# A hybrid S5 and gated-delta block on one Trainium2 core: S5 factors kept on chip, half of a copy on GpSimd, gate tiles queued behind read-outs

## The chip, the cores and the metric

The kernel runs on one core of one Trainium2 chip, in fp32 with fp32r and fp16 matmuls where the kernel splits values. The metric is device time in microseconds of one launch. Three runs of the kernel before gave 928.39, 932.23 and 933.82 us; their median is 932.23 us.

## The reference, cut to what matters

One layer: adaLN modulation, one input projection, two groups of heads, one output projection, LayerNorm. The change lies in the S5 group, which handles 512 of the 1024 mixed columns as 32 groups of 16 channels with 64 complex states, in two directions.

```
abar = exp(lam * dt);  bbar = ((abar - 1) / lam) * B          # per direction
h[t] = abar * h[t-1] + bbar @ u[t]                            # scan, started from the context's state
y    = d_skip * u + sum over both directions of Re(C @ h)
out  = glu(gelu(y)) * silu(z)                                 # z: the gate columns of the projection
```

The other group is a gated delta rule with a 3x3 convolution ahead of it and its own silu gate. The sequence has 1024 latent tokens after 256 context tokens.

## The kernel before, in words

The scan is cut into chunks of 8 tokens. Within a chunk the output is a Toeplitz product of the inputs (tile `m8`, built from kernels in DRAM `d_k`), and what comes from earlier chunks is the state at the chunk's edge (`ebuf`, copied to `hq`) times factors C·abar^t (tile `f`). Four S5 stages matter here:

- The **unfold** (lines 701 to 706, VectorE) completes the states in `ebuf`.
- The **Toeplitz stage** `s5_toeplitz` (lines 415 to 452), `t0` to `t3`, each for two quads of four groups. It loads packed coefficients `spq` from `d_sp`, makes `f` in six VectorE products a quad (`cplx_chunk`, lines 406 to 411), stores `f` to DRAM `d_f` (line 429), multiplies it with C on TensorE (line 442) into `ka` and `kb`, copies these to `ktt` and stores `ktt` to `d_k` (line 450).
- The **read-out** `y_stage` (lines 831 to 874), `y0` to `y3`, each for eight groups. It loads `m8` in eight pieces from `d_k` (line 837), `u8` (line 841) and two `fq` from `d_f` (line 845), copies the states to `hq` (line 848: the lower 64 partitions forwards, the upper 64 backwards in time), runs 24 fp32 matmuls into `py` (lines 854 to 856), the GELU on ScalarE (line 857), eight transposes `pg` and the copies to `gT`, stored to `d_g` (line 871).
- The **gate tiles** `z_tile` (lines 818 to 824), `z0` to `z7`. Each loads 128 columns of the input projection (`wrz`), splits them in high and low parts (`wtz`, lines 724 and 725), runs 48 matmuls of 128x512 (`pjz`, lines 142 to 144), and stores the silu (`csz`) to `d_z`.

After them come the GLU (`w`: its weights `wgr` split into `wgt`; `g`: matmuls `pgl`) and, in memory that the projection's operands leave, the delta-rule part, whose first instructions are `mg` on GpSimd (line 1188).

Order. The program is traced in an order written by hand, `ORD` (line 1103), and a planner then places each engine's instructions by priority in that order and by its own costs. `issue_after` puts the block's instructions behind a given one on that one's engine only. DMA issues stand in the queues of the engine that issues them (Q is SP, S is ScalarE), each in order. SBUF tiles share slots by tag: `kk`, `ra` and `ac` have two, `u4` four, `wr4` two, `w8` two (split projection weights), `y4` four. In the trace, slots of a tag are handed out in the order of the program. `ktt` and `csz` are in `kk`, `f` and `hq` in `ra`, the product's scratch, `ysb` and `gT` in `ac`, `spq` and the GLU's split weights in `u4`; `m8`, `u8` and `fq` are in `u4` for even and in `y4` for odd read-outs. `wrz`, `wgr` and the `zts` of the GLU use `wr4`.

Of the kernel before, what the change touches and what calls it, by code (L numbers as in the profile page):

```python
# [9 lines left out]
F32 = mybir.dt.float32  # L10
# [4 lines left out]
AF = mybir.ActivationFunctionType  # L15
# [4 lines left out]
P = 128  # L20
# [5 lines left out]
NG = 32  # L26
# [15 lines left out]
def tile_hybrid_block(  # L42
# [30 lines left out]
    V, S, G, T, Q = nc.vector, nc.scalar, nc.gpsimd, nc.tensor, nc.sync  # L73
# [12 lines left out]
    def bankE(nm):  # L86
        return psW.tile([P, 512], F32, tag="e", name=nm)
# [40 lines left out]
    d_uc = tc.dram_tile([CTX, 512], F32, name="d_uc")  # L128
    d_e = tc.dram_tile([P, NG, 2, P], F32, name="d_e")
    d_sp = tc.dram_tile([P, 8, 336], F32, name="d_sp")  # L130
    d_f = tc.dram_tile([P, NG, 2, P], F32, name="d_f")
    d_k = tc.dram_tile([NG, GC, 240], F32, name="d_k")
    d_kt = tc.dram_tile([HEADS, P, TOK], F32, name="d_kt")
    d_qkv = tc.dram_tile([3, HEADS, P, TOK], F32, name="d_qkv")
# [42 lines left out]
    def c5(shape, nm, tag):  # L177
        return cvp.tile(shape, F32, tag=tag, name=nm)
# [4 lines left out]
    def u4(nm, dt=F32, n=1024):  # L183
        return ld.tile([P, n], dt, tag="u4", name=nm, bufs=4)
# [214 lines left out]
    def cplx_chunk(cr, ci, pr, pi, conj, ch, tv, tg, E2):  # L399
        shp = [P, 4, 8, GC]  # L400
        cr, ci = bc(cr[:, :, None, :], shp), bc(ci[:, :, None, :], shp)
        pr = bc(pr.rearrange("p t g -> p g t")[:, :, :, None], shp)
        pi = bc(pi.rearrange("p t g -> p g t")[:, :, :, None], shp)
        vr = ch[:, :, 0, :].rearrange("p g (t c) -> p g t c", t=8)
        vi = ch[:, :, 1, :].rearrange("p g (t c) -> p g t c", t=8)
        V.tensor_tensor(vr, cr, pr, op=ALU.mult)
        V.tensor_tensor(tv, ci, pi, op=ALU.mult)
        V.tensor_tensor(vr, vr, tv, op=ALU.add if conj else ALU.subtract)
        E2.tensor_tensor(vi, ci, pr, op=ALU.mult)
        E2.tensor_tensor(tg, cr, pi, op=ALU.mult)  # L410
        E2.tensor_tensor(vi, vi, tg, op=ALU.subtract if conj else ALU.add)

    tz = {}

    def s5_toeplitz(q0, q1):
        for q in range(q0, q1):
            if q % 2 == 0:
                tz["k"] = c5([P, 2, 240], f"ktt{q}", "kk")
                tz["s"] = sq2 = u4(f"spq{q}", n=672)
                Q.dma_start(sq2, d_sp[:, q:q + 2].rearrange("p q f -> p (q f)"))  # L420
            kt = tz["k"]
            sq = tz["s"][:, (q % 2) * 336:(q % 2) * 336 + 336]
            ctt = [sq[:, 128 + 64 * i:192 + 64 * i].rearrange("p (j c) -> p j c", c=GC) for i in range(2)]
            fpp = [sq[:, 256 + 32 * i:288 + 32 * i].rearrange("p (t j) -> p t j", j=4) for i in range(2)]
            dd = sq[:, 320:336]
            f = c5([P, 4, 2, P], f"f{q}", "ra")
            ftmp = c5([P, 4, 8, GC], f"ft{q}", "ac")
            cplx_chunk(ctt[0], ctt[1], fpp[0], fpp[1], True, f, ftmp, ftmp, V)
            S.dma_start(d_f[:, q * 4:(q + 1) * 4], f)
            bank_ = bankW if q % 2 else bankE  # L430
            pa, pb = bank_(f"ka{q}"), bank_(f"kb{q}")
            for part in range(2):
                for lo, ps, cc0, f0, ft in ((0, pa, 0, 16, 0), (64, pb, 112, 0, 1)):
                    for ri in range(2):
                        for j in range(4):
                            w = sq[lo:lo + 64, 64 * ri + j * GC:64 * ri + j * GC + 32]
                            if part == 0:
                                o, m = ps[32 * j:32 * j + 32, cc0:cc0 + GC], ctt[ri][lo:lo + 64, j, :]
                            else:
                                o = ps[32 * j:32 * j + 32, f0:f0 + 112]  # L440
                                m = f[lo:lo + 64, j, ri, ft * GC:ft * GC + 112]
                            T.matmul(o, w, m, start=(ri == 0), stop=(ri == 1), tile_position=(lo, 32 * j))
            k2 = kt[:, q % 2, :]
            V.tensor_copy(k2[:, 128:240], pa[:, 16:128])
            V.tensor_tensor(k2[:, 112:128], pa[:, 0:16], dd, op=ALU.add)
            V.tensor_copy(k2[:, 0:112], pb[:, 0:112])
            V.tensor_tensor(k2[:, 112:128], pb[:, 112:128], k2[:, 112:128], op=ALU.add)
            if q % 2:
                for j in range(4):
                    S.dma_start(  # L450
                        d_k.rearrange("(q j) c f -> j c q f", j=4)[j][:, q - 1:q + 1], kt[32 * j:32 * j + GC],
                    )

# [254 lines left out]
    def chain(n0, n1):  # L708
        ar, ai = apw[2]
        for m in range(n0, n1, 4):  # L710
            prev, cur = ebuf[:, m - 4], ebuf[:, m]
            ta = rtp.tile([P, NG, 2], F32, tag="rta", name=f"rta{m}")
            tb = rtp.tile([P, NG, 2], F32, tag="rtb", name=f"rtb{m}")
            G.tensor_tensor(ta, prev, ar, op=ALU.mult)  # L714
            G.tensor_tensor(tb, prev[:, :, ::-1], ai, op=ALU.mult)
            G.tensor_tensor(ta, ta, cur, op=ALU.add)
            G.tensor_tensor(cur, ta, tb, op=ALU.add)
# [108 lines left out]
    d_g = tc.dram_tile([4, P, LAT], F32, name="d_g")  # L826
# [3 lines left out]

    def y_stage(ct):
        ysb = c5([P, 8, P], f"ysb{ct}", "ac")
        yt_ = u4 if ct % 2 == 0 else y4
        m8 = yt_(f"m8_{ct}").rearrange("p (g f) -> p g f", g=8)
        u8 = yt_(f"u8_{ct}").rearrange("p (g f) -> p g f", g=8)
        for s in range(8):
            Q.dma_start(
                m8[16 * s:16 * s + 16],
                d_k[ct * 8:ct * 8 + 8, :, (7 - s) * 16:(7 - s) * 16 + P].rearrange("g c f -> c g f"),
            )  # L840
        Q.dma_start(u8, d_ug[:, ct * 8:ct * 8 + 8])
        for q in range(2):
            g0 = ct * 8 + q * 4
            fq = yt_(f"fq{g0}").rearrange("p (g r f) -> p g r f", g=4, r=2)
            Q.dma_start(fq, d_f[:, g0:g0 + 4])
            hq = c5([P, 4, 2, P], f"hq{g0}", "ra")
            for lo, sl in ((0, slice(NCX - 1, NST - 1)), (64, slice(NST - 2, NCX - 2, -1))):
                S.activation(  # L848
                    hq[lo:lo + 64].rearrange("p g r n -> p n g r"), ebuf[lo:lo + 64, sl, g0:g0 + 4, :], AF.Copy,
                )  # L850
            py = bankE(f"py{g0}")
            for j in range(4):
                o = py[:, j * P:(j + 1) * P]
                T.matmul(o, u8[:, q * 4 + j], m8[:, q * 4 + j], start=True, stop=False)
                T.matmul(o, hq[:, j, 0, :], fq[:, j, 0, :], start=False, stop=False)
                ins = T.matmul(o, hq[:, j, 1, :], fq[:, j, 1, :], start=False, stop=True)
            S.activation(
                ysb[:, :, q * 64:(q + 1) * 64].rearrange("p t (g c) -> p g t c", c=GC),
                py.rearrange("p (g t c) -> p g t c", g=4, t=8), AF.Gelu,
            )  # L860
        gT = c5([P, LAT], f"gT{ct}", "ac")
        for h2 in range(2):
            pg = bankE(f"pg{ct}_{h2}")
            for j in range(4):
                T.transpose(pg[:, j * P:(j + 1) * P], ysb[:, h2 * 4 + j, :], ident)
            V.tensor_copy(
                gT.rearrange("p (n t) -> p t n", t=8)[:, h2 * 4:h2 * 4 + 4, :],
                pg.rearrange("p (t n) -> p t n", t=4),
            )
        if ct < 3:  # L870
            S.dma_start(d_g[ct], gT)
        else:
            marks["gT"] = gT
        return ins
# [221 lines left out]
    ebuf = epool.tile([P, NSL, NG, 2], F32, name="ebuf")  # L1096
# [3 lines left out]
        e_stage(hf)  # L1100
        fold(hf)
    chain(7, 35)
    ORD = "z0 t0 z1 z2 t1 y0 z3 t2 y1 z4 t3 y2 z5 y3 z6 w z7 g"
    for hd in range(HEADS):
        head(hd)
        if hd < 2:
# [8 lines left out]
    def y4(nm):  # L1115
        return yp.tile([P, 1024], F32, tag="y4", name=nm)
# [14 lines left out]
    marks = {}  # L1131
    for st in ORD.split():
        name, _, hold = st.partition(">")
# [308 lines left out]
    def gate_z(hd):  # L1442
        zt = gs.tile([P, LAT], F32, tag="zt", name=f"zt{hd}", bufs=1)
        Q.dma_start(zt, d_z[1, hd])
        return zt
# [195 lines left out]
    z3 = gate_z(HEADS - 1)  # L1641
# [37 lines left out]
```

## Time and profile before

| | |
|---|---|
| median of three runs | 932.23 us |
| the profiled execution | 937.24 us, its span 934.9 us |
| TensorE busy | 817.6 us (87%), mean clock 0.949 |
| VectorE, ScalarE, GpSimd busy | 668.6, 431.0, 372.5 us |
| HBM read, written | 85.53 MB, 41.23 MB |

Times on a timeline are microseconds from the span's start. The heads' convolutions end near 400; t0 to t3, y0 to y3 and the gate tiles lie between 379 and 539; the delta-rule part fills the rest. A matmul in fp32 over 128 columns appears as two instructions. The clock is the share of TensorE's full speed that was granted; a TensorE row's busy time overlaps the next one's start, so the distance of starts is the better price.

### The profile page before, as it was taken

The numbers are of one execution on the slowest core, as the hardware profiler recorded it, in microseconds if no ns is written. First come the engines' busy times: TensorE is split into PE (matmuls) and PEld (weight loads), VectorE is DVE, ScalarE is ACT, GpSimd is POOL, SyncE is SP. The second block draws the span as 40 slices with busy tenths as digits, with TensorE's granted clock in tenths as the row PEclk, the third lists the DMA queues.
The fourth block names the chain that finished last, engine by engine and source line by source line (L and its number), as shares of the span: only waits on it lengthen the run. The fifth ranks groups of instructions, "written<-read, shape, count | busy, mean of one in ns | idle before, by whom it ended". The sixth has DMA issues, their size and how long they took to land.

```text
span 934.9 us, 17192 instructions
## 1 busy us (share of the span) xinstructions
PE 817.6 (87%) x6553; PEld 675.7 (72%) x6553; DVE 668.6 (72%) x1318; ACT 431.0 (46%) x950; POOL 372.5 (40%) x455
## 2 busy tenths in 40 slices
PE   5987999997889999999894995799899989779994
PEld 2655897785776788877673884688777977677883
DVE  7977986996766778998432489677574765676576
ACT  1321435324434454421458475565743753456363
POOL 3224240007897930100000078875752773351063
PEclk9998999999898999999997897799999999899997
DMA  9980447412304323347546576421314224314423
GB/s 248 295 178 12 178 165 228 145 39 75 130 23 163 112 100 96 123 151 216 164 137 224 181 265 196 148 92 46 125 59 143 72 104 150 123 44 144 161 98 117
DMA packets 122427, 127.87 MB, mean 137 GB/s; under 512 B 21662, under 2 KB 95958, under 8 KB 122218
## 3 DMA queue, kind: packets, MB, share of 16 engines
q1 hardware_dynamic: 101898, 87.55, 32.5%
q10 hardware_dynamic: 20448, 39.23, 11.1%
q8 instruction: 52, 0.85, 0.4%
q14 instruction: 29, 0.24, 0.1%
HBM read 85.53 MB, written 41.23 MB: 136 GB/s over the span
## 4 chain that ended last, share of the span: by engine, by line
PE 53%; DVE 15%; DMA 13%; POOL 7%; ACT 5%; issue 5%; SPq 1%; ACTq 0%; POOLq 0%; DVEq 0%
PE pjz L142 3%; PE pjz L143 2%; PE pjz L144 2%; DMA xr<-in_x_dram 2%; PE pjk L142 2%; PE pjk L143 2%; PE pjk L144 2%; PE u L142 2%; DMA ml<-d_mix 2%; DMA kT<-d_qkv 2%; DMA wad<-in_w_ada_dram 2%; ACT hq L848 2%; PE pjv L143 2%; PE u L143 2%; PE pjv L144 2%
## 5 line engine op out<-in xcount | busy, mean ns | idle before, releaser
L1188 POOL TENSOR_TENSOR mg<-tri,ghi 128x512 fp32r<-128x512 f32 x20 | 23.1, 1157 | 196.9 <-PE pjz L144 153.9
L714 POOL TENSOR_TENSOR rta<-ebuf,ar 128x64 f32<-128x64 f32 x38 | 24.8, 653 | 85.4 <-DVE ebuf L689 82.6
L142 PE MATMUL pjz<-h_hi,wtz 128*128 128x512 f32 x128 | 52.1, 407 | 0.5 <-ACT csz L823 0.5
L143 PE MATMUL pjz<-h_lo,wtz 128*128 128x512 f32 x128 | 51.4, 402 | 0.0
L144 PE MATMUL pjz<-h_hi,wtz 128*128 128x512 f32 x128 | 51.1, 399 | 0.0
L1299 PEld LDWEIGHTS <-xz 128*128 128x128 f16 x480 | 37.2, 101 | 18.5 <-issue 12.4
L1283 DVE TENSOR_TENSOR pad<-pp,lvm 128x256 f16<-128x256 f32 x100 | 40.4, 416 | 13.1 <-PE pp L1275 12.5
L1299 PE MATMUL px<-pad,xz 128*128 128x64 f16 x480 | 42.0, 197 | 6.9 <-DVE pad L1283 5.3
L1312 DVE TENSOR_TENSOR xz<-px,xz 128x512 f16<-128x512 f32 x60 | 40.6, 684 | 9.7 <-PE px L1299 7.7
L760 DVE SCALAR_TENSOR_TENSOR cak<-crk,cwt,cak 128x945 f32<-128x945 f32 (+2 forms) x32 | 39.5, 1234 | 7.6 <-ACT cak L750 7.1
L1299 PE MATMUL px<-xz,pad 128*128 128x64 f16 x480 | 43.2, 197 | 0.0
L760 DVE SCALAR_TENSOR_TENSOR caq<-crq,cwt,caq 128x945 f32<-128x945 f32 (+2 forms) x32 | 39.2, 1224 | 5.0 <-ACT caq L750 3.1
L760 DVE SCALAR_TENSOR_TENSOR cav<-crv,cwt,cav 128x945 f32<-128x945 f32 (+2 forms) x32 | 39.8, 1243 | 3.7 <-ACT cav L750 3.4
L1275 PE MATMUL pp<-xz,t 128*128 128x64 f16 x480 | 33.7, 197 | 8.0 <-DVE xz L1312 3.5
L848 ACT ACTIVATE hq<-ebuf 64x1024 f32<-64x1024 f32 x16 | 31.9, 1991 | 13.0 <-DMA d_k<-ktt 8.4
L804 POOL TENSOR_TENSOR kss<-kss,mhalf 128x4 f32<-128x4 f32 (+1 forms) x12 | 15.6, 1307 | 55.1 <-DVE kss L803 55.1
L1275 PEld LDWEIGHTS <-t 128*128 128x128 f16 x480 | 27.9, 101 | 13.1 <-issue 11.5
L142 PE MATMUL u<-wu,h_lo 128*128 128x512 f32 x64 | 29.9, 468 | 8.3 <-DVE h_lo L563 8.3
L1400 ACT ACTIVATE uu<-s 128x128 f32<-128x128 f32 x80 | 20.7, 278 | 31.1 <-PE s L1396 27.6
L1396 PE MATMUL s<-rr,zf 128*128 128x128 f32 x144 | 30.7, 303 | 4.1 <-DVE rr L1391 4.0
L1310 ACT ACTIVATE xz<-px 128x512 f16<-128x512 f32 x40 | 23.6, 595 | 23.0 <-PE px L1299 17.5
L557 ACT ACTIVATE hraw<-xt,ss 128x512 f32<-128x512 f32 (+1 forms) x24 | 15.8, 702 | 37.1 <-DVE ss L545 18.0
(513 smaller groups left out, 2997.7 us busy)
## 6 DMA issues: line engine op xcount, KB each, us to landing
wad<-in_w_ada_dram SPq DMA_DIRECT2D x16, 512.0 KB, 6.6
xk<-in_x_dram SPq DMA_DIRECT2D x8, 512.0 KB, 6.7
d_e<-et ACTq DMA_DIRECT2D x8, 512.0 KB, 3.1
etl<-d_e SPq DMA_DIRECT2D x8, 512.0 KB, 4.3
wg<-in_w_ada_dram SPq DMA_DIRECT2D x8, 512.0 KB, 6.2
wrz<-in_w_in_dram SPq DMA_DIRECT2D x8, 512.0 KB, 3.8
d_z<-csz ACTq DMA_DIRECT2D x8, 512.0 KB
d_f<-f ACTq DMA_DIRECT2D x8, 512.0 KB, 4.1
```

The costliest lines, as they stand in the source:

```text
L142: T.matmul(ps, ll, rh, start=first, stop=False)
L143: T.matmul(ps, lh, rl, start=False, stop=False)
L144: return T.matmul(ps, lh, rh, start=False, stop=last)
L714: G.tensor_tensor(ta, prev, ar, op=ALU.mult)
L760: clast[typ, hd] = V.scalar_tensor_tensor(out=o, in0=rv[:, y0 + dy:y1 + dy, x0 + dx:x1 + dx], scalar=cwt[:, t, (dy + 1) * 3 + dx + 1:(dy + ...
L848: S.activation(hq[lo:lo + 64].rearrange("p g r n -> p n g r"), ebuf[lo:lo + 64, sl, g0:g0 + 4, :], AF.Copy,)
L1275: T.matmul(pp[:, u * 64:(u + 1) * 64], t16[:, u, :], cols(xs[u], b, u // 2), start=True, stop=True)
L1283: V.tensor_tensor(scat(pad[:, 0, :], b, 256, 128 // b), pp[:, :256].rearrange("p (d n b) -> p d n b", d=2, b=b), lvm[:, l - 1].rearrange(" ...
L1299: ins = T.matmul(o, lt, rt, start=not on_act, stop=not on_act or w == 3 and i == 1)
L1310: S.activation(xo, pxv, AF.Copy)
L1312: V.tensor_tensor(xo, pxv, xo, op=ALU.add)
L1396: ins = T.matmul(p2_[:, :P], hs["zf"][cp][:, d, i, :], rr, start=True, stop=True)
```

## The change

The factors `f` are made in `u4` tiles, kept in a table `fqs`, and read by the read-out from there: `d_f`, its stores and its loads go. `spq` moves from `u4` into one `kk` tile with `ktt`. The stores to `d_k` and `d_g` go from ScalarE's queue to SP's. The upper half of each `hq` is copied by GpSimd. `m8` and `u8` always use `y4`. In the order, `z4` to `z7` stand behind the last matmul of `y0` to `y3` on TensorE.

```diff
 def s5_toeplitz(q0, q1):
             if q % 2 == 0:
-                tz["k"] = c5([P, 2, 240], f"ktt{q}", "kk")
-                tz["s"] = sq2 = u4(f"spq{q}", n=672)
+                sk = c5([P, 1152], f"spq{q}", "kk")
+                tz["k"] = sk[:, 672:].rearrange("p (q f) -> p q f", q=2)
+                tz["s"] = sq2 = sk[:, :672]
                 Q.dma_start(sq2, d_sp[:, q:q + 2].rearrange("p q f -> p (q f)"))
...
-            f = c5([P, 4, 2, P], f"f{q}", "ra")
+            f = fqs[q] = u4(f"f{q}").rearrange("p (g r f) -> p g r f", g=4, r=2)
             ftmp = c5([P, 4, 8, GC], f"ft{q}", "ac")
             cplx_chunk(ctt[0], ctt[1], fpp[0], fpp[1], True, f, ftmp, ftmp, V)
-            S.dma_start(d_f[:, q * 4:(q + 1) * 4], f)
...
-                    S.dma_start(
+                    Q.dma_start(
                         d_k.rearrange("(q j) c f -> j c q f", j=4)[j][:, q - 1:q + 1], kt[32 * j:32 * j + GC],
 def y_stage(ct):
-        yt_ = u4 if ct % 2 == 0 else y4
-        m8 = yt_(f"m8_{ct}").rearrange("p (g f) -> p g f", g=8)
-        u8 = yt_(f"u8_{ct}").rearrange("p (g f) -> p g f", g=8)
+        m8 = y4(f"m8_{ct}").rearrange("p (g f) -> p g f", g=8)
+        u8 = y4(f"u8_{ct}").rearrange("p (g f) -> p g f", g=8)
...
-            fq = yt_(f"fq{g0}").rearrange("p (g r f) -> p g r f", g=4, r=2)
-            Q.dma_start(fq, d_f[:, g0:g0 + 4])
+            fq = fqs[g0 // 4]
...
-                S.activation(
-                    hq[lo:lo + 64].rearrange("p g r n -> p n g r"), ebuf[lo:lo + 64, sl, g0:g0 + 4, :], AF.Copy,
-                )
+                dst, src = hq[lo:lo + 64].rearrange("p g r n -> p n g r"), ebuf[lo:lo + 64, sl, g0:g0 + 4, :]
+                if lo:
+                    G.tensor_copy(dst, src)
+                else:
+                    S.activation(dst, src, AF.Copy)
...
-            S.dma_start(d_g[ct], gT)
+            Q.dma_start(d_g[ct], gT)
...
-    ORD = "z0 t0 z1 z2 t1 y0 z3 t2 y1 z4 t3 y2 z5 y3 z6 w z7 g"
+    ORD = "z0 t0 z1 z2 t1 y0 z3 t2 z4>y0 y1 t3 z5>y1 y2 z6>y2 y3 w z7>y3 g"
```

## Rows read from the trace of the kernel before

**Rows 1.** Windows, 403.6 to 539.1 and its emptiest part: length, busy us of engines, clock, DMA

```profile
403.60:539.10 135.50, 115.72 (x1000) 92.62 (x1001) 71.28 (x122) 61.34 (x57) 0.03 (x1) 0.90 0.55 176
...
489.80:527.60 37.80, 23.00 (x211) 19.88 (x211) 12.49 (x24) 26.51 (x24) 0.00 (x0) 0.73 0.67 218
```

**Rows 2.** Windows of the gate matmuls (pjz) alone: PE, PEld and ACT busy, clock, DMA

```profile
370.00:442.20 72.20, 58.30 (x233) 42.30 (x233) 4.44 (x8) 1.00 0.50 165
...
489.80:527.60 37.80, 0.15 (x1) 0.12 (x1) 2.17 (x4) 0.73 0.67 218
...
527.60:539.10 11.50, 11.15 (x48) 8.89 (x48) 0.82 (x2) 1.00 0.30 116
```

**Rows 3.** Chain of waits, 489 to 528: shares by line

```profile
by line: DMA d_f<-f 25.7%; ACT hq L848 16.1%; DMA graw<-d_g 9.2%; DMA wgr<-in_w_glu_dram 7.9%; issue 6.8%; PE py L854 5.3%; PE py L856 4.4%; PE py L855 4.4%; DVE gT L866 3.6%; ACT L857 3.3%; PE pgl L142 1.9%; DVE wgt L878 1.8%; DVE f L408 1
```

**Rows 4.** Waits, 440 to 540: waiter, what ended it, us, times, longest

```profile
ACT L823 <- DMA d_g<-gT: 11.0, 1, 11.0
...
ACT hq L848 <- DMA d_k<-ktt: 8.4, 1, 8.4
```

**Rows 5.** Timeline of GpSimd, 239 to 241 and at 539: start, us, instruction, idle before

```profile
239.66 0.32 POOL L715 TENSOR_TENSOR rtb<-ebuf,ai 128x64 f32<-128x64 f32 x1
...
239.94 1.22 POOL L716 TENSOR_TENSOR rta<-rta,ebuf 128x64 f32<-128x64 f32 x1
...
539.07 1.05 POOL L1188 TENSOR_TENSOR mg<-tri,ghi 128x512 fp32r<-128x512 f32 x1 [153.92 <-PE pjz L144]
```

**Rows 6.** DMA issues, 400 to 545: issuer, count, KB each, median us to landing

```profile
d_f<-f ACTq DMA_DIRECT2D x8, 512.0 KB, 4.1
...
u<-d_ug SPq DMA_DIRECT2D x4, 512.0 KB, 7.3
...
spq<-d_sp SPq DMA_DIRECT2D x2, 336.0 KB, 5.3
...
d_k<-ktt ACTq DMA_DIRECT2D x16, 30.0 KB, 1.9
```

**Rows 7.** Instruction groups of ScalarE, 380 to 545: count, busy us, mean ns, idle before

```profile
L848 ACT ACTIVATE hq<-ebuf 64x1024 f32<-64x1024 f32 x16 | 31.9, 1991 | 13.0 <-DMA d_k<-ktt 8.4 <-DMA d_f<-f 2.9 <-PE kb L442 1.6
```

**Rows 8.** Instruction groups of GpSimd, whole span, shapes apart

```profile
L497 POOL TENSOR_TENSOR wu<-wur,wu 128x1024 fp32r<-128x1024 f32 x4 | 9.6, 2409 | 43.3 <-ACT wu L496 43.3
```

**Rows 9.** Timeline of SP's queue: issues merged

```profile
306.36 4.82 SPq L420 DMA_DIRECT2D spq<-d_sp  x2
...
503.37 4.12 SPq L837 DMA_DIRECT2D m<-d_k  x8
```

**Rows 10.** Timeline of TensorE, at 402, 501 to 506 and 524 to 528

```profile
401.87 1.84 PE L781 MATMUL pqq<-ones,q2q 128*128 128x1 f32 x16
...
501.27 0.80 PE L855 MATMUL py<-fq,hq 128*128 128x128 f32 x2 [5.11 <-ACT hq L848]
...
505.67 0.39 PE L856 MATMUL py<-fq,hq 128*128 128x128 f32 x2
...
524.44 0.39 PE L854 MATMUL py<-m,u 128*128 128x128 f32 x2
...
524.89 0.39 PE L856 MATMUL py<-fq,hq 128*128 128x128 f32 x2
...
527.70 0.39 PE L142 MATMUL pjz<-h_hi,wtz 128*128 128x512 f32 x1
```

**Rows 11.** Timeline of VectorE: last unfold instruction, and a product of t2

```profile
441.54 0.43 DVE L689 TENSOR_TENSOR ebuf<-ebuf 128x256 f32<-128x256 f32 x1
...
458.90 0.69 DVE L406 TENSOR_TENSOR f<-spq 128x512 f32<-128x512 f32 x1 [6.08 <-DMA spq<-d_sp]
```

**Rows 12.** Windows of the Toeplitz matmuls (line 442) after 454.7: PE, PEld, clock, DMA

```profile
454.70:527.60 72.90, 6.07 (x256) 3.22 (x256) 0.81 0.55 179
```

**Rows 13.** Timeline of ScalarE: z2's first half leaves; the last GLU weight splits

```profile
415.87 0.60 ACT L823 ACTIVATE csz<-pjz 128x512 f32<-128x512 f32 x1 [4.33 <-DMA d_z<-csz]
...
517.94 1.15 ACT L877 ACTIVATE wgt<-wgr 128x512 fp32r<-128x512 f32 x2
```

More of the change, by code (lines that the diff above doesn't have):

```diff
@@ L130, in tile_hybrid_block @@
     d_sp = tc.dram_tile([P, 8, 336], F32, name="d_sp")
-    d_f = tc.dram_tile([P, NG, 2, P], F32, name="d_f")
     d_k = tc.dram_tile([NG, GC, 240], F32, name="d_k")
@@ L411, in cplx_chunk @@
         E2.tensor_tensor(vi, vi, tg, op=ALU.subtract if conj else ALU.add)
-    tz = {}
+    tz, fqs = {}, {}
     def s5_toeplitz(q0, q1):
```

## The prediction

> **What bounds the kernel now.** I read the windows by stretch first, then the chain of waits, then the waits, then each engine's timeline. From 403.6 to 539.1 TensorE is busy 115.7 of 135.5 us: 19.8 us idle, and a mean clock of 0.90; 14.8 of the idle us lie between 489.8 and 527.6, at clock 0.73 [rows 1]. The reader is to see there that no other engine is full either, so this is a stage of waits. The windows of the gate tiles alone show why it is empty: 233 of their 384 matmuls have gone by 442.2, one runs between 489.8 and 527.6, and the last tile's 48 follow in 11.15 us [rows 2]. The planner has used the cover early, and the last two read-outs stand bare. In that stretch the chain gives 25.7% of 39 us (10 us) to the stores d_f<-f and 16.1% to the hq copies [rows 3]: the copy needs the "ra" slot that the factors leave only when their store has landed. ScalarE's queue is further held by stores that wait for VectorE, 11.0 us at one d_g and 8.4 us at one d_k [rows 4]. GpSimd's next stage starts at 539.07, released by the last gate matmul after 153.92 us of idleness [rows 5]. So a microsecond off the end of z7 is a microsecond off the kernel, and I price the change by when z7 ends.
>
> **The change, part by part.**
>
> *Factors on chip.* Eight d_f stores of 512 KB [rows 6] and the eight fq loads of the same bytes go; the factors now stay in four u4 slots, f4 and f5 taking those of y0. The "ra" tag is left to hq, so the 10 us of rows 3 go. What is late next there is hq itself.
>
> *Stores on SP.* Sixteen d_k and three d_g issues leave ScalarE. On SP the loads of m8 stood behind the landing of the same d_k anyway, so the wait at the head of SP's queue is not new; what queues behind it are weights loaded a tile ahead. I take 0; ScalarE loses its 8.4 and 11.0 us of waits [rows 4], which come back only as readiness, not as a term.
>
> *Half of hq on GpSimd.* ScalarE's copy is 1.99 us, 16 of them, so 8 leave it: 15.9 us [rows 7]. No row shows GpSimd copying 64x1024. From below, half of the two-input 128x1024 row, 1.2 us; from above, 16 times 0.32 us for 64 elements, 5.1 us [rows 5, 8]. I take 2.4 us, the two-input row itself, because strides cost something and the second input is saved. GpSimd is idle here. The two halves go side by side, so a pair costs 2.4 instead of 4.0 us, and only y0's first pair is bare.
>
> *Load of the factors' inputs moved.* This part costs. Spq was fetched at 306.36, far ahead, in u4 [rows 9]; now it shares one "kk" tile with ktt, two slots, taken in the order of the program behind z0. The slot comes when head 3's q2q has been read, about 404 [rows 10]. From there: 5.3 us load [rows 6], twelve products of 0.69 us [rows 11], 8.3 us alone and about 22 with an unfold instruction between every two (I take 15), 3.5 us for the matmuls and ktt (an estimate from the matmul windows of rows 12 and the four small copies), 1.8 + 1.9 us for d_k, 4.1 us to issue eight m8 loads [rows 9], then u8, 7.3 us [rows 6]. Sum 38.9, so y0 could start at 443. The other gate is the unfold, done at 442.0 [rows 11], plus the 2.4 us pair: 444.4. Start of y0: 444, bounds 437 (t1's products late, so the unfold ends about 8 us sooner, held by u8) and 450 (22 us for 15).
>
> *Gate tiles held.* Four tiles are 192 matmuls; 233 had run by 442.2, so about 41 of z4 are pushed behind y0: 41/48 of 11.15 = 9.5 us. TensorE runs out of gate work at 432.7 and waits some 11 us for y0, less t1's matmuls. I charge this gap in full. After 5.11 us of idleness ten py pairs took 4.40 us, 501.27 to 505.67, against 0.225 us each at the end of y3 [rows 10]: the granted clock in that stretch is 0.73 [rows 1], a mix of its 2.4 and 1.2 GHz levels; so y0 pays 10 x 0.215 = 2.2 us more.
>
> *The last gate tile's weights.* The GLU weights take wr4 slots ahead of z7's, and wait for u4 slots that f6 and f7 hold until y3. Before, from the first of the last two weight splits (517.94) to z7's first matmul (527.70) is 9.8 us [rows 10, 13]. After, that split can start when y3's first half is done, 2.7 us before its end, so z7 starts up to 7.1 us after y3; before it was 2.8 us (524.89 to 527.70). I take 6.
>
> *Sum from y0's start at 444, TensorE without other gaps:* y0 24 x 0.225 + 2.2 = 7.6; z4 to z6 33.5; y1 to y3 16.2; eight pg transposes three times, some 1.1 each (eight by 0.11, as a py instruction, and their fill) 3.3; t2 and t3 6.1 [rows 12]; gap 6.0; z7 11.2. That is 83.9, so z7 ends at 527.9 instead of 539.1: 11.2 us less. The profiled execution took 937.24 us (span 934.9 and 2.3 around it), 5.0 over the median 932.23; it would take 926.0, and the median 921.0. What follows 539 has the same work and the same starter, so I move it whole.
>
> One rule speaks against GpSimd here. The chain on GpSimd shows it: the same 128x64 form takes 0.32 us and, in the next instruction, 1.22 us [rows 5]. The Trainium skill, "SBUF — State Buffer", section "Who interferes with whom", says that a VectorE instruction with two SBUF inputs and a GpSimd instruction that reads SBUF lock each other out, the second waiting for the whole of the first; the trace agrees, as far as a fourfold time can show it. By that rule copies and products would not overlap; what it does to the time is rival 2.
>
> **Rivals.**
>
> 1. *Slower: the factors' slot comes late, and the held tiles can't cover.* Place: the first "kk" load. Every us that it is later than 404 moves y0 once the sum above passes 444; with 38.9 us behind it, z7 ends where it did if the load goes at 416, and 0.5% later if at 421. The next slot is z1's, which ScalarE waited for until 415.87 [rows 13]; that gives 455 and no change. If t0 gets only z2's slot, about 7.5 us on (z2's second half, and a landing like z1's, which ScalarE waited 4.33 us for [rows 13]), y0 starts at 462, z7 ends at 546: 939. For it: the tag has two slots and eight gate tiles use them. Against: q2q's slot is free first, and only z0 is ahead.
>
> 2. *GpSimd and VectorE in each other's way.* t1's products end with the unfold, about 443, so y1 is ready 18.6 us later, about 462 (matmuls, d_k, m8, u8), and its place behind z4 is 444 + 7.6 + 11.2 = 463. Four copies of 2.4 to 5.1 us among those products make it 9.6 to 20 us less a part that overlaps; I take 3 to 9 us of bare wait: 924 to 930. For: 1 us of slack. Against: the copies would mostly come after those products. It would turn the sign only at 10 us a copy, a pair per period of 20 us.
>
> 3. *The gain is given back at z7.* TensorE finds GLU matmuls ready before z7's weights and runs one half, 48 at 0.23 = 11 us, ahead of it. Then the next stage starts where it did and only the GLU's part is won: 926 to 933. For: one pgl pair already stands just ahead of z7. Against: those need y3's own transposes.
>
> 4. *The same plan, better.* The unfold ends early, y0 starts at 438, z7's weights cost 3: 9 us more, 912.
>
> That the change doesn't do what it says would show as d_f gone but hq still waited for; I count it with 3.
>
> **How the numbers follow.** Forecast 0.42 (917 to 927), rival 4 0.14 (907 to 917), rival 2 0.16, rival 3 0.16, rival 1 0.12. Faster by over 0.5% (4.7 us, about what a measurement of this kernel can tell from none; below 927.6): 0.42 + 0.14 + 0.11 of rival 2 + 0.05 of rival 3 = 0.72. Within it: 0.05 + 0.11 + 0.02 of rival 1 = 0.18. Slower: 0.10. Leaving out the worse part of rival 1 and the best tail of rival 4, the range is 907 to 933.
>
> **What would show it.** In the changed profile: no d_f; sixteen hq halves, eight on each engine, at 2 to 3 us on GpSimd; 48 gate matmuls behind each read-out; one TensorE gap of about 11 us just before the first py, then idleness under 15 us to the end of z7; GpSimd's mg released by pjz near 528. A first spq load after 416, a bare wait before y1, or pgl rows ahead of z7 would show rivals 1, 2 and 3. The forecast is wrong if z7 ends after 535, or if it ends near 528 and the total doesn't follow.

## The result, and the profile after

The changed kernel took 922.22 us (median of 7 runs, 919.21 to 926.23) against 933.82 us for the kernel before on the same chip: ratio 0.987, 95% interval 0.984 to 0.990. A second set gave 0.983 (0.980 to 0.987), without one of its six runs, 959.69 us at a mean clock of 0.82, which fell in a slower state of the chip. The change is faster by 1.3 to 1.7%; the forecast was 921.0 us, 1.2% under the median shown.

The profiled execution took 919.21 us, its span 917.5. Line numbers behind the removed `d_f` are one lower than before (the GpSimd half of hq has line 847, ScalarE's half 849). First the windows: the whole stage from 403.6, which answers to the first of [rows 1], then its two empty places and the full part between them. Columns: length, busy us of TensorE, its weight loads, VectorE, ScalarE and GpSimd with their counts, granted clock, DMA share, GB/s.

```profile
403.60:528.05 124.45, 105.78 (x1011) 86.65 (x1010) 76.35 (x123) 45.88 (x50) 16.40 (x8) 0.90 0.43 127
430.00:443.50 13.50, 3.37 (x68) 2.09 (x68) 10.70 (x22) 3.79 (x4) 2.67 (x2) 0.53 0.64 176
450.50:507.40 56.90, 56.90 (x537) 47.88 (x537) 30.72 (x49) 26.91 (x28) 10.59 (x6) 1.00 0.43 123
507.40:516.60 9.20, 4.81 (x20) 3.66 (x19) 6.22 (x8) 5.59 (x8) 0.00 (x0) 0.78 0.89 306
```

The idleness has not shrunk much over the stage (18.7 us, 19.8 before), and it is no longer spread over y2 and y3: one hole of 10.1 us before y0, then 56.9 us with TensorE busy for all of them at clock 1.00, then a hole before z7. What shrank is TensorE's busy time. The next windows run from the last head transposes to the delta-rule part, before and after; the second of each pair has the read-outs' matmuls (py) alone, with TensorE, its weight loads and ScalarE.

```profile
388.99:539.07 150.08, 130.30 (x1097) 104.64 (x1096) 85.79 (x138) 67.32 (x66) 0.00 (x1) 0.91 0.55 178
388.99:539.07 150.08, 29.46 (x192) 27.58 (x192) 4.76 (x8) 0.91 0.55 178
```
```profile
386.25:528.05 141.80, 123.03 (x1100) 101.14 (x1099) 92.23 (x140) 52.36 (x60) 16.40 (x8) 0.92 0.44 134
386.25:528.05 141.80, 25.85 (x192) 24.70 (x192) 4.76 (x8) 0.92 0.44 134
```

Of the 8.3 us by which this stretch is shorter, 1.0 is idleness (19.8 to 18.8) and 7.3 are busy time. 3.6 of these are the same 192 read-out matmuls, of which fewer ran at the half-clock spacing of 0.43 us, and 1.6 are seven gate matmuls that now run ahead of the stretch (331 start in it instead of 338, 0.23 us each); the rest is not divided here. So most of what this stretch won is work done faster or earlier, not idle time filled.

Two timelines of TensorE show the holes' ends; columns are start, us, instruction, count, and in brackets the idle time before and what ended it.

```profile
436.69 0.41 PE L441 MATMUL ka<-f,spq 64*32 64x112 f32 x4 [6.79 <-DVE f L410]
441.36 0.77 PE L853 MATMUL py<-m,u 128*128 128x128 f32 x2 [3.44 <-DMA spq<-d_sp]
443.50 0.79 PE L854 MATMUL py<-f,hq 128*128 128x128 f32 x2
444.09 0.64 PE L855 MATMUL py<-f,hq 128*128 128x128 f32 x2
...
447.50 0.52 PE L854 MATMUL py<-f,hq 128*128 128x128 f32 x2
...
507.37 0.39 PE L855 MATMUL py<-f,hq 128*128 128x128 f32 x2
508.45 1.09 PE L864 MATMUL pg<-ident,ysb 128*128 128x128 f32 x8 [0.69 <-ACT ysb L856]
513.24 1.22 PE L141 MATMUL pgl<-g_hi,wgt 128*128 128x512 f32 x2 [3.70 <-ACT g_hi L876]
514.26 0.63 PE L141 MATMUL pjz<-h_hi,wtz 128*128 128x512 f32 x1
514.69 0.63 PE L142 MATMUL pjz<-h_lo,wtz 128*128 128x512 f32 x1
```

Before y0 TensorE waits 6.8 us for t1's last factor products on VectorE and 3.4 us for y0's data (the trace names spq's load, the same place in a later kernel u8's, which is issued at 436.65 below). Nothing waits for a factor's store any more. At z7 the starts are 0.43 us apart for twelve matmuls, where z7 before ran in the 11.15 us of [rows 2].

The next fence has the two timelines that answer to [rows 9] and to the last row of [rows 5]: SP's loads of the factors' inputs, m8 and u8 of y0, and GpSimd's copies and its release into the delta-rule part.

```profile
399.36 0.34 SPq L420 DMA_DIRECT2D spq<-d_sp  x1
...
428.25 1.96 SPq L449 DMA_DIRECT2D d_k<-spq  x4
...
432.69 3.91 SPq L835 DMA_DIRECT2D m<-d_k  x8
436.65 0.43 SPq L839 DMA_DIRECT2D u<-d_ug  x1
```

```profile
440.83 3.72 POOL L847 COPY hq<-ebuf 64x1024 f32<-64x1024 f32 x2 [58.46 <-DVE ebuf L688]
448.41 4.69 POOL L847 COPY hq<-ebuf 64x1024 f32<-64x1024 f32 x2 [3.86 <-PE py L855]
...
528.05 1.05 POOL L1187 TENSOR_TENSOR mg<-tri,ghi 128x512 fp32r<-128x512 f32 x1 [35.34 <-PE pjz L143]
```

GpSimd's delta-rule work starts at 528.05 (539.07 before). But the span fell by 17.4 us, not by 11.0. The windows from that start to the end of the span, for the two traces of each kernel (before, before again, the change, the change again), show where the rest is; the columns are the same as above.

```profile
539.07:934.90 395.83, 338.69 (x3358) 292.41 (x3356) 271.57 (x611) 216.18 (x579) 217.91 (x247) 0.94 0.38 123
```
```profile
535.84:933.10 397.26, 339.76 (x3358) 293.61 (x3356) 271.87 (x611) 216.25 (x579) 218.73 (x247) 0.95 0.37 123
```
```profile
528.05:917.50 389.45, 339.77 (x3358) 292.57 (x3356) 270.49 (x611) 215.03 (x579) 219.79 (x247) 0.94 0.38 125
```
```profile
527.97:916.20 388.23, 336.34 (x3358) 290.13 (x3356) 273.85 (x611) 215.24 (x579) 219.53 (x247) 0.95 0.38 126
```

The same 3358 matmuls with nearly the same busy time and clock: what differs is TensorE's idleness, 57.1 and 57.5 us before, 49.7 and 51.9 after.

### The profile page after: what moved, and what is told of

Same layout as the page of the kernel before. It is cut to its first block, busy times and chain, and to the rows that moved or that the text cites. A ratio compares the mean times of both kernels' runs of the same rounds, so it can differ in the third digit from the quotient of the medians.

```text
span 917.5 us, 17187 instructions
## 1 busy us (share of the span) xinstructions
PE 814.1 (89%) x6553; PEld 674.8 (74%) x6553; DVE 672.5 (73%) x1318; ACT 415.2 (45%) x944; POOL 392.1 (43%) x463
## 5 line engine op out<-in xcount | busy, mean ns | idle before, releaser
L847 POOL COPY hq<-ebuf 64x1024 f32<-64x1024 f32 x8 | 16.4, 2068 | 93.9 <-DVE ebuf L688 58.5
L1390 DVE SCALAR_TENSOR_TENSOR rr<-s,ngx,vt 128x128 f32<-128x128 f32 x72 | 24.5, 344 | 17.0 <-PE s L1386 16.4
L822 ACT ACTIVATE csz<-pjz 128x512 f32<-128x512 f32 x16 | 9.2, 597 | 54.9 <-PE pjz L143 43.0
```

The lines of the kernel that those rows point to most:

```text
L1390: V.scalar_tensor_tensor(out=rn, in0=p1_[:, :P], scalar=ngx[:, d, ch, hd:hd + 1], in1=rr, op0=ALU.mult, op1=ALU.add,)
```

## The experiments

All traces are cut at two marks: the start of the last two transposes of the heads (pkTk), and the first `mg` on GpSimd. Between them lies the S5 stage, behind them the delta-rule part. Idle is length less TensorE's busy time; ratios are to the kernel before, timed beside each kernel.

| kernel | S5 stage, us | idle in it | delta-rule part, us | idle in it | ratio (95%) |
|---|---|---|---|---|---|
| before | 150.1 | 19.8 | 395.8 | 57.1 | |
| before, again | 148.5 | 17.9 | 397.3 | 57.5 | |
| order alone | 147.6 | 22.5 | 390.4 | 52.1 | 0.993 (0.990 to 0.996) |
| factors alone | 144.6 | 19.8 | 394.2 | 53.1 | 0.988 (0.983 to 0.993) |
| all but the order | 145.3 | 19.9 | 389.9 | 51.6 | 0.989 (0.985 to 0.993) |
| factors and order | 144.5 | 20.6 | 388.6 | 50.8 | 0.986 (0.982 to 0.990) |
| the change, hq on ScalarE | 142.8 | 19.8 | 393.7 | 54.6 | 0.988 (0.984 to 0.992) |
| the change, stores on ScalarE | 141.7 | 19.3 | 388.3 | 50.2 | 0.985 (0.982 to 0.988) |
| the change | 141.8 | 18.8 | 389.5 | 49.7 | 0.987 (0.984 to 0.990) |
| the change, again | 141.7 | 19.5 | 388.2 | 51.9 | 0.983 (0.980 to 0.987) |
| before, tags swapped | 160.0 | 26.4 | 390.4 | 50.5 | 1.003 (1.000 to 1.006) |
| z7 ahead of the GLU | 133.8 | 14.8 | 387.4 | 48.8 | 0.977 (0.973 to 0.981) |
| that, and z4 free | 132.1 | 13.0 | 386.0 | 50.4 | 0.974 (0.970 to 0.978) |

The stretch ahead of the first mark ends between 384.6 and 392.3 in these thirteen traces, with both of before (389.0, 387.3) inside that band. The work there is nearly the same in all of them, so I take differences there as scatter between executions. The interval of a ratio is about 0.4% to either side, 4 us, so parts of 3 us are told apart by the traces, not by the times; a part of the stage under 1.6 us, by which the two traces of before differ, isn't told apart at all.

**Order alone.** The kernel before, with the new `ORD` and nothing else.

```diff
-    ORD = "z0 t0 z1 z2 t1 y0 z3 t2 y1 z4 t3 y2 z5 y3 z6 w z7 g"
+    ORD = "z0 t0 z1 z2 t1 y0 z3 t2 z4>y0 y1 t3 z5>y1 y2 z6>y2 y3 w z7>y3 g"
```

> The kernel before with the new order alone (z4 to z7 behind y0 to y3); factors still go through DRAM, both hq halves and all stores on ScalarE. Theory (both parts are needed): the held tiles cover part of the waits for the factors' stores and for hq, but with hq still behind them in ScalarE's queue some stay bare; the gate's last matmul ends at 532 to 536 on the timeline instead of 539 and the ratio to before is 0.992 to 0.998. Rival a (the order is all of it): end near 528, ratio 0.985 to 0.990. Rival b (the factors on chip are all of it): ratio 1.00 or more, since the gap before y0 of 10 us is added and nothing is won.

Measured: the stage 147.6 us, the last gate matmul's end at 535.5, ratio 0.993: as the theory had it by both numbers, though the end alone says little, since before's second trace has it at 535.84. The waits from 436 on (waiter, what ended it, us in total, times, longest) show what holding tiles can't cover:

```profile
PE py L855 <- ACT hq L848: 19.6, 5, 9.0
ACT L823 <- DVE f L411: 19.1, 2, 9.7
...
ACT hq L848 <- DMA d_k<-ktt: 8.1, 1, 8.1
...
ACT hq L848 <- DMA d_f<-f: 0.8, 2, 0.4
```

TensorE waits 19.6 us for hq in the middle of its read-outs, where no gate tile may run. ScalarE is late with hq because its queue stands at stores: 19.1 us until VectorE has made factors that a d_f store is to take (the row names the silu of line 823, which stands behind that store) and 8.1 us at d_k; the landing of a d_f store is put down for 0.8 us. In the stage the order alone is worth 1.7 us against the mean of the two traces of before (149.3), hardly more than the 1.6 by which these differ; most of what its total gained lies behind the stage, which I did not yet see.

**All but the order.** The change with the old `ORD`.

```diff
-    ORD = "z0 t0 z1 z2 t1 y0 z3 t2 z4>y0 y1 t3 z5>y1 y2 z6>y2 y3 w z7>y3 g"
+    ORD = "z0 t0 z1 z2 t1 y0 z3 t2 y1 z4 t3 y2 z5 y3 z6 w z7 g"
```

> The changed kernel with the old order: gate tiles are not held, all else is changed. Theory (both parts are needed): the gate tiles run early again, y2 and y3 stand bare and wait for m8 and u8, so z7 ends at 533 to 537 and the ratio to before is 0.993 to 0.998. Rival a (the order is all of it): ratio 0.998 to 1.005. Rival b (the factors are all of it): z7 ends near 528, ratio 0.985 to 0.990.

Measured: the release at 532.95, at the early edge of the theory's range (533 to 537), but the ratio 0.989 is better than it allowed; it is that of rival b, whose end near 528 the trace doesn't have. So on top of the rest the order gives 3.5 us of stage (145.3 to 141.8), and the total says that something else was won too.

**Factors alone.** Factors in u4, spq with ktt in kk, m8 and u8 in y4; the rest as before.

```diff
-                if lo:
-                    G.tensor_copy(dst, src)
-                else:
-                    S.activation(dst, src, AF.Copy)
+                S.activation(dst, src, AF.Copy)
...
-            Q.dma_start(d_g[ct], gT)
+            S.dma_start(d_g[ct], gT)
```

(from the change, with the d_k stores and `ORD` put back too.)

> The factors in u4 tiles and spq in kk with ktt, m8 and u8 in y4; old order, both hq halves and the stores on ScalarE. Theory: without d_f the hq copies no longer wait for its stores (10 us of the chain in the emptiest stretch), but y2 and y3 still stand bare behind ScalarE's queue: ratio to before 0.994 to 1.000, and 0.3 to 0.6% behind the kernel that has the other parts too. Rival b (the factors are all of it): 0.985 to 0.990. Rival d (the later spq slot costs more than the stores did, where nothing covers it): 1.002 to 1.010.

Measured: ratio 0.988, which is what the rival that gives the factors everything asked for, not my 0.994 to 1.000. The trace sides with neither: its release is at 534.98 and the stage has 144.6 us, 4.7 better than before and 2.9 behind the change. Two bare waits stand in it:

```profile
505.23 1.97 PE L861 MATMUL pg<-ident,ysb 128*128 128x128 f32 x8 [6.12 <-ACT ysb L853]
...
520.65 1.22 PE L141 MATMUL pgl<-g_hi,wgt 128*128 128x512 f32 x2 [5.15 <-ACT g_hi L873]
```

With the order added (factors and order, below) the first is 0.7 us; the second stays, with 3.7.

**The change again.** The same kernel, for a second trace.

> The changed kernel once more, for a second trace and a second interval. If what was won outside the stage (2.8 us ahead of the third Toeplitz copy, 6.4 us behind the last gate matmul) is a property of the kernel, both stretches have the same length in this trace to 1 us and the ratio is 0.984 to 0.990; if it is scatter between executions, the stretch behind the last gate matmul is 392 to 398 us long here instead of 389.5.

Measured: 388.2 us behind the release (1.2 less than in the first trace, where 1 was allowed), 141.7 us of stage, ratio 0.983. The shorter delta-rule part belongs to the kernel, not to one execution.

**Before again.** The same kernel as before, for a second trace.

> The kernel before once more, for a second trace of it. In the first, 389.0 us lie ahead of the last head transpose, 150.1 to the first delta-rule instruction and 395.8 behind it; in the two of the changed kernel 386.3, 141.7 and 388.2 to 389.5. If what differs outside the stage is scatter between executions, the outer stretches are shorter here (386 to 388 and 388 to 393) and the middle one is 149.5 to 151; if it belongs to the kernel, all three are as in the first trace to 1 us.

Measured: 387.3, 148.5 and 397.3 us. The stretch ahead of the stage moved as scatter would, and so did the stage by 1.6 us; the delta-rule part did not get shorter. Each expectation is wrong in a part; the part that mattered says that some 6 to 9 us of the change's gain lie behind the stage, where no line of the program was edited.

**Factors and order, without the copies and stores.** Both hq halves and both stores back on ScalarE.

```diff
-                if lo:
-                    G.tensor_copy(dst, src)
-                else:
-                    S.activation(dst, src, AF.Copy)
+                S.activation(dst, src, AF.Copy)
...
-                    Q.dma_start(
+                    S.dma_start(
                         d_k.rearrange("(q j) c f -> j c q f", j=4)[j][:, q - 1:q + 1], kt[32 * j:32 * j + GC],
...
-            Q.dma_start(d_g[ct], gT)
+            S.dma_start(d_g[ct], gT)
```

> The changed kernel with both hq halves and the stores to d_k and d_g back on ScalarE: factors on chip and held gate tiles alone. From the last head transpose to the delta-rule part's first GpSimd instruction the traces so far have 150.1 us (before), 147.6 (order alone), 144.6 (factors alone), 145.3 (all but the order) and 141.8 and 141.7 (the change). Theory: the two parts add up, and the GpSimd copies and the queue of the stores are worth nothing to the end: this stretch 141 to 143 us, ratio to before 0.983 to 0.988. Rival (once the tiles are held, a shorter hq and a free ScalarE queue are what lets the read-outs be ready): 144 to 147 us, ratio 0.988 to 0.993.

Measured: 144.5 us, the rival's number; the total (0.986) can't tell. The timelines of TensorE and of ScalarE give the place, in y0:

```profile
450.20 0.80 PE L851 MATMUL py<-f,hq 128*128 128x128 f32 x2 [2.60 <-ACT hq L846]
```
```profile
444.42 1.73 ACTq L449 DMA_DIRECT2D d_k<-spq  x4
446.25 7.87 ACT L846 ACTIVATE hq<-ebuf 64x1024 f32<-64x1024 f32 x4 [8.55 <-DMA d_k<-spq]
```

ScalarE reaches its first hq only behind the four d_k issues, which stand in its queue ahead of it, and then copies four halves one after the other.

**Each of these two by itself.** The change with both hq halves on ScalarE (first part of that diff), and the change with the stores on ScalarE (its other two parts).

> The changed kernel with both hq halves on ScalarE; the stores stay on SP. Without both this and the stores' move the S5 stage took 144.5 us instead of 141.7 and 141.8. Theory (the copy on GpSimd is what those 2.8 us are): 143.5 to 145.5 us, with a wait for hq of 2 to 4 us inside y0, and the total 0.1 to 0.4% behind the changed kernel. Rival (the stores are what matters): 141 to 142.5 us and no wait for hq over 1 us. Rival (VectorE and GpSimd disturb each other, so that the copies cost as much as they save): 140 to 141.5 us.

> The changed kernel with the stores to d_k and d_g on ScalarE's queue again; the upper hq halves stay on GpSimd. Theory (the queue of these stores is worth nothing, as the prediction had it): S5 stage 141 to 142.5 us, ratio to before equal to that of the changed kernel within its interval. Rival: 143.5 to 145.5 us, since ScalarE's half of hq and its GELU stand behind stores that wait for VectorE.

Measured: 142.8 us, between the theory's and the rival's range, with a wait for hq of 0.66 us where I expected 2 to 4; and 141.7 us. So with the other part in place the copy on GpSimd is worth 1.1 us by this trace, less than the scatter of 1.6, and the stores' move nothing; only without both are 2.8 us lost. Either one lets y0's states be ready when its m8 and u8 are. The parts don't add up, they need each other: on top of the factors alone (144.6) the order gives nothing (144.5) and the copies and stores give nothing (145.3), both together 2.9 us.

**The delta-rule part's order.** In the change, the planner orders the delta-rule part differently on every engine, 419 of VectorE's 610 positions from the first mg on hold another instruction than before. One tag swap in the kernel before makes that order, instruction for instruction on TensorE, VectorE, ScalarE and GpSimd, the one of the change:

```diff
-        yt_ = u4 if ct % 2 == 0 else y4
+        yt_ = u4 if ct % 2 else y4
```

> The kernel before with the tags of m8, u8 and fq swapped: u4 for odd and y4 for even read-outs. The S5 stage is as before (factors through DRAM, no held tiles), but the planner then orders VectorE's and GpSimd's work in the delta-rule part exactly as in the changed kernel, where before it orders it differently. TensorE stood idle for 57.1 and 57.5 us behind the last gate matmul in the two traces of before, and for 49.7 to 53.0 in the seven kernels with another order. Theory (the order of the delta-rule part is what won there): idle 49 to 53.5 us, that stretch 388 to 394 us long instead of 395.8 and 397.3, the S5 stage 147 to 152 us as before, ratio to before 0.989 to 0.996. Rival (less traffic or an earlier end of the S5 stage shortened it, so that it belongs to the change proper): idle 56 to 58 us, 395 to 398 us long, ratio 0.998 to 1.004.

Measured, from its first mg to its end:

```profile
547.95:938.40 390.45, 339.93 (x3358) 292.92 (x3356) 272.42 (x611) 215.08 (x579) 220.14 (x247) 0.94 0.38 125
```

390.4 us, 50.5 of them idle: the theory's numbers, with an S5 stage that is nothing like the change's. That stage got 10 us longer through the swap (160.0, expected 147 to 152), so the total is 0.3% behind before and not ahead of it; the expectation failed there. Five traces have this order exactly (the change twice, factors alone, stores on ScalarE, tags swapped): 388.2 to 394.2 us, 49.7 to 53.1 idle. Two have the order of before: 395.8 and 397.3, 57.1 and 57.5 idle. So it is the order that shortens this part, not the edited stage ahead of it. The margin is small in one trace, 394.2 against 395.8; that one, factors alone, is the slowest of its six runs (931.67 us, their median 925.18). The loads in SP's queue change places with the engines' order, 15 of 117 in each of these five traces, so the two orders aren't told apart; why TensorE idles less is left open.

**z7 ahead of the GLU's weights.**

```diff
-    ORD = "z0 t0 z1 z2 t1 y0 z3 t2 z4>y0 y1 t3 z5>y1 y2 z6>y2 y3 w z7>y3 g"
+    ORD = "z0 t0 z1 z2 t1 y0 z3 t2 z4>y0 y1 t3 z5>y1 y2 z6>y2 y3 z7>y3 w g"
```

> The changed kernel with the last gate tile traced ahead of the GLU's weights, so that its own weights have their slots first. In the changed kernel TensorE is empty for 6.7 us after y3 and then runs twelve matmuls at half clock (some 2.4 us). Theory (this gap is the z7 weights' wait for GLU weights, and z7's end sets the next stage): no gap over 2 us ahead of z7, the stretch to the first delta-rule instruction 133 to 137 us, ratio to before 0.974 to 0.981. Rival (given back: the GLU's matmuls and weights now come after z7 and stand in the delta-rule part's way): the stretch shortens as said but the part behind it grows by 4 us or more, ratio 0.982 to 0.988.

Measured: 912.83 us, ratio 0.977, stage 133.8, and 387.4 us behind it: nothing was given back. Its windows over the place before y0 and over z7:

```profile
430.00:443.50 13.50, 3.71 (x69) 2.44 (x70) 9.89 (x21) 4.60 (x4) 3.48 (x2) 0.50 0.71 191
507.20:519.30 12.10, 12.10 (x58) 10.00 (x58) 5.65 (x8) 5.59 (x9) 0.00 (x0) 1.00 0.57 181
```

The hole and the half clock at z7 go when the GLU's weights stand behind the last gate tile: 8.0 us of the stage.

**That, and z4 free.**

```diff
-... t2 z4>y0 y1 t3 z5>y1 y2 z6>y2 y3 w z7>y3 g"
+... t2 z4 y1 t3 z5>y1 y2 z6>y2 y3 z7>y3 w g"
```

> As the kernel with z7 ahead of the GLU, and the fourth gate tile not held behind y0, so that it can fill the 10 us in which TensorE waits for y0. Theory (the read-outs' pace is set by the chain spq slot, factors, d_k, m8, u8, some 20 us per read-out, so that a gate tile spent before y0 is missing later): the gap before y0 goes and one of 6 to 10 us appears before y2, and the kernel is within 0.4% of the one with z7 alone ahead. Rival (TensorE's work is the bound once the gap is filled): 8 to 10 us less than that kernel, ratio to before 0.965 to 0.972.

Measured: 910.92 us, ratio 0.974 to the 0.977 of the kernel above, which the intervals (0.970 to 0.978 and 0.973 to 0.981) do not separate. TensorE now works through 430 to 447, and the hole comes back before y1 instead of y2:

```profile
430.00:447.20 17.20, 15.46 (x187) 12.12 (x186) 17.16 (x31) 4.44 (x5) 1.19 (x1) 1.00 0.45 126
454.50:466.70 12.20, 4.13 (x74) 2.72 (x73) 9.01 (x13) 6.66 (x7) 2.26 (x2) 0.61 0.66 201
```

Filling a hole by moving a cover moved the hole, as the theory said; the place was wrong. This kernel has the lowest median of all that I ran.

## Why the prediction was right, and where it was wrong

**The bound.** Right: the delta-rule part starts when z7 ends, in all thirteen traces, and z7 ended at 528.05 and 527.97 for a forecast of 527.9. Only 8.3 us of this are the stage, though (150.1 to 141.8; 7.6 between the means of two traces each), since the heads happened to end 2.7 us sooner.

**Factors on chip.** The d_f waits of [rows 3] went. With the new order and ScalarE's queue as before, TensorE waits 19.6 us for hq where the factors go through DRAM and 2.6 us where they stay on chip. The prediction put this cost on the "ra" slot, which waits for a store's landing; in the order alone most of it is the d_f stores themselves, at which ScalarE's queue stands until their factors are made. The forecast put the 10 us that go to this part; by itself it shortened the stage by 4.7. It also is what the planner's other order came with, since that kernel has it exactly.

**Slot and y0's start.** The first spq load was issued at 399.36, for 404 forecast: 1.9 us early once the heads' 2.7 us are taken off. y0 started 55.1 us behind the last head transpose, for 444 - 389.0 = 55.0. Its chain has 42.0 us for 38.9: spq, products, matmuls and ktt took 28.9 (399.36 to 428.25) for 23.8, d_k 4.4 for 3.7, m8 4.0 for 4.1, and u8 4.7 (436.65 to 441.36) for 7.3. The unfold, done at 440.7, and the first pair of hq were not late. The start is right because these errors cancel.

**Half of hq on GpSimd.** 2.4 us forecast, 2.07 the mean of eight, and 1.93 where it ran undisturbed beside ScalarE's half. Its worth, 1.6 us forecast for y0's pair, is 1.1 by the trace without it, within the scatter.

**Stores on SP.** Taken as 0, and 0 they are by themselves.

**Gate tiles held.** The hole before y0 was charged with 11 us and has 10.1, and behind it eight py pairs start 0.43 us apart (444.09 to 447.50), as after the gap of [rows 10]. From 450.5 to 507.4 the sum assumed no gap, and there is none. What the trace showed too late: the order needs hq to be ready, by the factors and by one of the two relieved queues, or the gap reappears inside the read-outs.

**The gap before z7.** 6.0 us forecast, 6.9 measured as the forecast counted its 2.8 before, from the start of y3's last matmuls (507.37) to z7's first (514.26). The sum forgot that TensorE then comes out of a hole, as at y0: with twelve matmuls at 0.43 us instead of 0.23, z7 takes 13.8 us to the release of GpSimd, where before it took 11.4. From y0's start to that release it is 86.7 us for 83.9. The same rows that priced y0's slow start would have priced this.

**What follows 539.** "I move it whole" is the step that failed. The part behind the stage is 6.4 to 9.0 us shorter in either trace of the change than in either of before, and the runs show why: its instructions are the same, their order is not. So the forecast of the median came out right by luck, by two errors of opposite sign: the stage gave 8 us for 11, and the delta-rule part 7 or so for 0. In the two profiled pairs this makes 15, and 17 with the earlier heads; the medians differ by 12 and 14, since both profiled runs of the change lie below its median and both of before above theirs.

**The rivals.** The first, a late slot, did not come: 399, not 416. The third, GLU matmuls ahead of z7, is there with one pair of pgl, as before, and not with a half. The second is in the trace, without its price. VectorE's instructions beside GpSimd's copies, and then the eight copies together (shortest, median and longest in ns):

```profile
448.29 0.69 DVE L405 TENSOR_TENSOR f<-spq 128x512 f32<-128x512 f32 x1 [7.59 <-PE py L855]
448.89 2.30 DVE L408 TENSOR_TENSOR f<-spq 128x512 f32<-128x512 f32 x1
451.12 2.35 DVE L405 TENSOR_TENSOR f<-spq 128x512 f32<-128x512 f32 x1
...
471.51 1.26 DVE L405 TENSOR_TENSOR f<-spq 128x512 f32<-128x512 f32 x1 [4.17 <-DMA spq<-d_sp]
...
490.80 2.28 DVE L877 TENSOR_TENSOR wgt<-wgr,wgt 128x512 fp32r<-128x512 f32 x1 [4.96 <-ACT wgt L876]
493.65 0.69 DVE L877 TENSOR_TENSOR wgt<-wgr,wgt 128x512 fp32r<-128x512 f32 x1 [0.57 <-ACT wgt L876]
```
```profile
L847 POOL COPY hq<-ebuf x8: 1931/2008/2419, 440.8 to 490.7; 64x1024 f32<-64x1024 f32 x8
```

Two products took 2.30 and 2.35 us instead of 0.69 while GpSimd copied (448.41 to 453.10), and those two copies 4.69 us together, where y0's first two, undisturbed, took 3.72. The copy at 470.37 held a third product (1.26 us), and the one at 490.67 the split of a GLU weight (2.28 us; the next, without a copy beside it, 0.69). In the kernel with both halves on ScalarE the longest of the sixteen products of lines 405 and 408 has 0.70 us. So a product waited out most of a copy, which is what the Trainium skill, "SBUF — State Buffer", section "Who interferes with whom", says of a VectorE instruction with two SBUF inputs beside a GpSimd instruction that reads SBUF. No cost of it shows at the end: y1 stands behind 48 gate matmuls, and TensorE has no gap from 450.5 to 507.4.

## What to carry to other kernels

Cover that is spent early is missing late: find where the last independent work ran out, and hold it back, but only once nothing inside the covered stretch waits for another queue. When a planner orders the program, an edit in one stage can reorder an untouched one; compare two traces of each kernel behind the stage, and the instruction order there, before giving its microseconds to the edit. Parts that each win nothing on top of one may win together, so try them in pairs before dropping one. And price what comes behind a hole on TensorE too: behind both holes here the work started at half clock.

## What the runs showed of the hardware

A VectorE product of 0.69 us, with two SBUF inputs, took 2.30 to 2.35 us beside a GpSimd copy that reads SBUF, and the copy itself up to 2.42 for 1.93 us; in the kernel with all copies on ScalarE, whose copies have the same shape, the products of the same two lines stayed at 0.70 us at most. The clock fell on both holes: granted 0.53 from 430.0 to 443.5 (10.1 us idle) and 0.78 from 507.4 to 516.6 (4.4 us idle), a mix of the 1.2 and 2.4 GHz levels, and the matmuls behind either hole had nearly double spacing (0.43 for 0.23 us); in the kernel whose z7 follows y3 at once it stayed at 1.00.
